# A decoder block in fp32: the raw weights of the third block get a pair of tiles of their own, in the place of a part of h2 that no product reads

## The chip, the cores and the metric

The kernel runs on one core of a Trainium2 chip. A core has a matrix engine (TensorE, PE), a vector engine (VectorE, DVE), an activation engine (ScalarE, ACT), a general engine (GpSimd, POOL) and an engine that here only issues transfers (SyncE, SP), all with their own queue of instructions, which is worked through in order. They wait for each other on semaphores. Data lies in an on-chip memory of 128 partitions (SBUF); matmuls write into banks of a second one (PSUM). The metric is the device time of one execution in microseconds (us); less is better.

## The reference

The input x has 512 tokens of width 1024. One layer:

```python
h = rmsnorm(x, norm_attn_g)
u_q, u_k, u_v, u_pool, u_gate = split(h @ w_in)
a = diff_attention(u_q, u_k, u_v, positions, lam, subln_g)
p = multiscale_pool(u_pool, w_pool, pool_scale)
gates = sigmoid(u_gate)
x = x + (gates[0] * a + gates[1] * p) @ w_out
h2 = rmsnorm(x, norm_mlp_g)
z = square(relu(h2 @ w_up))          # w_up: 1024 x 4096
x = x + z @ w_down                   # w_down: 4096 x 1024
return rmsnorm(x, final_norm_g)
```

All of it is fp32, and the result has to agree with a fp32 computation.

## The kernel before

Each fp32 operand of a large product is split into a high part, a cast to the matrix engine's float32r, and a low part, the rest of it. A product is then three matmuls: high with high, high with low, low with high. A weight tile of 128 x 1024 is loaded by SP into a raw tile, cast by ACT (`split_w`, line 112), and DVE subtracts the cast from the raw tile (line 113). High parts lie in tiles named `wh`, low parts in `wl`, four of each in rotation; every third weight of the MLP uses two others.

The first 303 us are projections, attention and pooling, and up to 353 us the product with `w_out`. The rest is the MLP, in four quarters q = 0 to 3 of the hidden width. A quarter has a product `up` (line 718), which gives z, and a product `down` (line 801), which is added to x. Both are done by Strassen's scheme in Winograd's form: the operands are cut into 2 x 2 blocks, and seven products of half the size take the place of eight. The seven forms of an operand are called A11, A12, A22 and the sums S1, S2, S3, S4. The block A21 has no product of its own: it only goes into the sums.

- For `up`, the left operand is h2. `gab[0]` holds the high and low part of A11, and in its second half those of A21; `gab[1]` holds A12 and A22; `gss` holds the sums. The loop at line 616 takes both column blocks of each of the four token tiles (t = 0 to 3), casts them (ACT, L618) and subtracts (DVE, L619). So t = 2 and 3 with b = 0 give A21. The sums are made from other tiles (`hw`, `h2f`), by `forms_h2`.
- For `down`, the left operand is z. `zsplit` casts a form of z on ACT (L705) and subtracts on DVE (L708), from tiles (`rawz`) that ACT's L757 and L758 (relu, square) and DVE's L753 have made.
- The weights come from `weights` (line 632). Of the four blocks of a quarter, three are used in raw form: r11 (b = 0), b21 (b = 2, for form A12) and b22 (b = 3, for form S4). `raw` loads each as two tiles of 128 x 1024 (512 KB each) into tiles of the tag `wr`, of which there is one pair. So the load of b21 has to wait until r11 has been cast and subtracted, and that of b22 until b21 has. The sums of blocks, `ga` and `al` (tiles `wga`, `wal`), are made by DVE (L673) and by transfers of POOL that add to the tile which they write (L643). Weights made of them are named `wh_dt` and `wh_ut`; those of raw blocks `wh_db` and `wh_ub` (d for down, u for up).
- `parts` takes a `hold`: an instruction behind which the cast is put. For b11 and b21 of `down` it is the cast of z in form S1.
- In the last quarter, b22's low part is made in another way: ACT casts (L659) and negates (L660), and POOL adds the block from memory (L661).

The order of the instructions on each engine is set by a scheduler ahead of the run, from the dependences, the tiles that come free, and a few ordering hints (`after`). SP issues all raw loads in one queue, so a load that waits for its tile stands ahead of all later ones.

`xl`, the low part of the normed x in the first projections, lies in the same memory (slot s1) that `gab[0]` takes later.

Of the kernel before, what the change touches and what calls it, by code (L numbers as in the profile page):

```python
# [18 lines left out]
P = 128  # L19
S = 512  # L20
# [31 lines left out]
def block_kernel(ctx, tc, xT, x_tok, gains, pos, consts, w_in, w_v, w_pool, w_out, w_up, w_dn, out):  # L52
# [74 lines left out]
    def mm3(acc, hi, lo, rh, rl):  # L127

        for k in range(NK):
            c = slice(k * P, (k + 1) * P)  # L130
            T.matmul(acc, lhsT=hi[:, c], rhs=rh[:, k, :], start=k == 0, stop=False)  # L131
            T.matmul(acc, lhsT=hi[:, c], rhs=rl[:, k, :], start=False, stop=False)  # L132
        for k in range(NK):
            c = slice(k * P, (k + 1) * P)
            T.matmul(acc, lhsT=lo[:, c], rhs=rh[:, k, :], start=False, stop=k == NK - 1)  # L135
# [8 lines left out]
    subc = con[:, 56:57]  # L144
    posi = cf.tile([P, NT], I32, name="posi")
    xh = B16(0, F32R, "xh")
    xl = B16(1, F32R, "xl")

    ident = cp.tile([P, P], F32, name="ident")
    make_identity(nc, ident)  # L150
# [24 lines left out]
    def xprep(k):  # L175
        xt = gt0[:, k % 4, :]
        nc.sync.dma_start(out=xt, in_=xT[k])
        A.activation(out=xh[:, k, :], in_=xt, func=AF.Copy, scale=g1c[:, k : k + 1])
        V.scalar_tensor_tensor(
            out=xl[:, k, :], in0=xt, scalar=g1c[:, k : k + 1], in1=f(xh)[:, k, :],  # L180
            op0=ALU.mult, op1=ALU.subtract,
        )

# [18 lines left out]
    for n in range(2):  # L202
        accs = [bank(4 * n + t, f"v{n}_{t}") for t in range(NT)]
        for kk in range(4):
            if n == 0:
                xprep(2 * kk)
            if n == 0 and kk == 0:
                raw, hi, lo = wv0
                nc.sync.dma_start(out=raw[:, 512:], in_=w_v[0, 0, :, 512:])
            else:  # L210
                raw, hi, lo = load_w(w_v[n, kk], f"v{n}_{kk}", 2 if n == 0 else 1)
            for k2 in range(2):
                if n == 0 and k2 == 1:
                    xprep(2 * kk + 1)
                sl = slice(k2 * 512, k2 * 512 + 512)
                split = split_w(raw, hi, lo, sl, eng=V)
                k = 2 * kk + k2
                for t in range(NT):
                    tsl = slice(t * P, t * P + P)
                    T.matmul(accs[t], lhsT=xh[:, k, tsl], rhs=hi[:, sl], start=k == 0, stop=False)  # L220
                    T.matmul(accs[t], lhsT=xh[:, k, tsl], rhs=lo[:, sl], start=False, stop=False)  # L221
                    T.matmul(accs[t], lhsT=xl[:, k, tsl], rhs=hi[:, sl], start=False, stop=k == NK - 1)  # L222
                if n == 0:
                    after(xsquare(k), split)
        if n == 0:
            pr = bank(4, "pr")
            T.matmul(pr, lhsT=ones, rhs=ssx, start=True, stop=True)
            rsqrt(rb, pr, tmp("sq", "nt1"), D)
            A.mul(out=rb, in_=rb, mul=-0.5)
            pc = bank(5, "pc")  # L230
            for t in range(NT):
                T.matmul(pc[:, 2 * t : 2 * t + 2], lhsT=ssx[:, t * P : t * P + P], rhs=ones[:, 0:2], start=True, stop=True)
            rct = cf.tile([P, NT, 2], F32, name="rct")
            rsqrt(rcol, pc[:, 0:8].rearrange("p (a b) -> p a b", a=NT), rct, D)
            A.mul(out=rcol, in_=rcol, mul=-0.5)
        for t in range(NT):
            vd = [v_[:, 4 * n : 4 * n + 4, t * P : t * P + P] for v_ in (vh, f(vh), vl)]
            av = accs[t].rearrange("p (h d) -> p h d", h=4)
            A.activation(out=vd[0], in_=av, func=AF.Copy, scale=rcol[:, t, 0:1])
            V.scalar_tensor_tensor(  # L240
                out=vd[2], in0=av, scalar=rcol[:, t, 0:1], in1=vd[1],
                op0=ALU.mult, op1=ALU.subtract,
            )
# [276 lines left out]

    h2f = zf("h2f", F32)

    gab = [big.tile([P, 2, 2, 4, HS], F32R, tag=f"s{i}", name=f"gab{i}") for i in (1, 4)]
    gss = [big.tile([P, 2, 2, 4, HS], F32R, tag=f"s{i}", name=f"gss{i}") for i in (2, 3)]
    gf = {}
    for form, g_, j in ((A11, gab[0], 0), (A12, gab[1], 0), (A22, gab[1], 1), (S1, gss[0], 0), (S2, gss[0], 1), (S3, gss[1], 0), (S4, gss[1], 1)):
# [68 lines left out]
    for t in range(NT):  # L595
        a_ = bank(4 + t, f"po1_{t}")
        for k in range(NK):
            mm_rows(a_, t, k, ws[k // 2], k == 0, k == NK - 1)
        x1_add(t, 1, a_)
        V.scalar_tensor_tensor(out=h2[:, t % 2], in0=x1[:, t, :], scalar=row_scale(t, 1), in1=g2b, op0=ALU.mult, op1=ALU.mult)  # L600
        pv = []
        for b in range(2):
            pt = bank((t % 2) * 2 + b, f"h2T{t}_{b}")
            for j in range(4):
                k = 4 * b + j
                state["h2T"] = T.transpose(out=pt[:, j * P : j * P + P], in_=h2[:, t % 2, k * P : k * P + P], identity=ident)
            pv.append(pt.rearrange("p (j q) -> p j q", q=P))
        sl = slice((t % 2) * P, (t % 2) * P + P)
        if t > 1:

            A.copy(out=hw[:, 1, :, sl], in_=pv[0])
            V.tensor_tensor(out=hw[:, 0, :, sl], in0=pv[1], in1=hw[:, 1, :, sl], op=ALU.subtract)
            forms_h2((S1, S2), sl)
        if t == 3:
            forms_h2((S3,), slice(0, HS))
        for b in range(2):
            hi, lo = (gab[b][:, t // 2, i, :, sl] for i in range(2))
            A.copy(out=hi, in_=pv[b])  # L618
            part = V.tensor_tensor(out=lo, in0=pv[b], in1=f(hi), op=ALU.subtract)  # L619
            if t == 3:  # L620
                after(part, state[S3])
            if t < 2:
                A.copy(out=h2f[:, b, :, sl], in_=pv[b])
# [8 lines left out]
    def weights(src, q, nm, order):  # L632

        def raw(b, tag="wr", pool=wp):
            tiles = [pool.tile([P, 1024], F32, tag=tag, name=f"{tag}_{nm}{b}_{q}_{c}", bufs=2) for c in range(2)]
            if b is not None:
                for c in range(2):
                    nc.sync.dma_start(out=tiles[c], in_=src[q, b, c])
            return tiles

        def plus(tiles, b):

            return [G.dma_start(out=tiles[c], in_=src[q, b, c], accum_op=ALU.add) for c in range(2)]  # L643

        def parts(rs, b, hold=None, add=None):

            third = nparts[0] % 3 == 2
            nparts[0] += 1
            out_ = []
            for c in range(2):  # L650
                hi, lo = (
                    (bk if third else wp).tile([P, 1024], F32R, tag=t_ + "b" * third, name=f"{t_}_{nm}{b}_{q}_{c}", bufs=2 if third else 4)
                    for t_ in ("wh", "wl")
                )
                if add is None:
                    cast = split_w(rs[c], hi, lo, eng=V)
                else:

                    cast = A.copy(out=hi, in_=rs[c])  # L659
                    A.mul(out=lo, in_=f(hi), mul=-1.0)  # L660
                    G.dma_start(out=lo, in_=src[q, add, c], accum_op=ALU.add)  # L661
                if hold:
                    after(cast, hold)
                out_.append((hi, lo))
            return out_

        early = nm == "u" and q == 0
        r11, al, ga = raw(0), raw(1, "wal", bk), raw(None, "wga", bk)
        for c in range(2):
            if early:  # L670
                nc.sync.dma_start(out=ga[c], in_=src[q, 0, c])
            else:
                V.tensor_tensor(out=ga[c], in0=r11[c], in1=al[c], op=ALU.add)  # L673
        if early:
            plus(ga, 1)
            plus(al, 3)
        for n, form in enumerate(order):
            if form == A11:
                yield parts(r11, "b11", zhi[q, S1] if nm == "d" and q else None)
            elif form == A12:  # L680
                yield parts(raw(2), "b21", zhi[q, S1] if nm == "d" else None)
            elif form == S4:
                yield parts(raw(3), "b22", None, 3 if nm == "d" and q == 3 else None)
            elif form == S3:
                yield parts(al, "t3", first[-1])
            else:
                w = parts(ga, f"t{form}", state["rows"] if form == S1 and early else None if form == S1 else first[-1])
                if form != A22:
                    adds = plus(ga, {S1: 3, S2: 2}[form])
                if form == S1 and not early:  # L690

                    for i in plus(al, 3):
                        after(i, adds[1])
                yield w
# [271 lines left out]
```

## Time and profile before

| what | us |
|---|---|
| runs (three) | 687.55, 687.97, 690.27 |
| median | 687.97 |
| the profiled execution's own time | 693.66 |
| its span, first to last instruction | 691.9 |

The mean clock that was granted to TensorE in the profiled execution is 0.992 of full speed. A page of the profile gives busy times and shares of the span of each engine. The weight loads of the matrix engine (PEld) run beside its matmuls. `L112` in a row is line 112 of the kernel, and the names behind it are the tiles: out, an arrow, in. Two products of `up` with different blocks have the same line; the tiles tell them apart. Rows of the timeline give the start in us from the start of the span, the duration, and in brackets the idle time of the engine ahead of the row and what ended it. What ends an idle time is inferred from semaphores; where several are waited for, the row names one of them.

### The profile page before, as it was taken

To read this page: it belongs to the slowest core of one execution; us is meant where nothing else is said; L and a number is where in the kernel's file an instruction comes from. 1 tells how busy PE (TensorE), PEld (TensorE's weight loads), DVE (VectorE), ACT (ScalarE), POOL (GpSimd) and SP (SyncE) were. 2 spreads that over 40 slices of the span, in tenths; PEclk is the share of its full clock that TensorE was granted. 3 is DMA by queue.
4 is the path that set the end of the run, shared out by engine and by line. 5 is a ranking of instruction groups with operands and counts; after the bars stand their busy time and mean duration, and the time that the engine had idled before them with its cause. 6 is when DMAs were issued, how large, how long until landed. Compare 5 with 4: busy or idle time off the path is not lost.

```text
span 691.9 us, 10006 instructions
## 1 busy us (share of the span) xinstructions
PE 670.4 (97%) x3686; PEld 581.5 (84%) x3686; DVE 516.8 (75%) x847; ACT 460.0 (66%) x741; POOL 171.1 (25%) x169
## 2 busy tenths in 40 slices
PE   8999999999999999999999999999999999989985
PEld 7788878887888888888889988999789987989764
DVE  6953977688778865965578999468894789646875
ACT  7554487877888688874578766366734776357665
POOL 6101634265346525510211020302111011202020
PEclk9999999999999999999999999999999999999998
DMA  8534473426345274564948486958669487675873
GB/s 271 180 121 114 131 152 108 112 63 153 98 124 137 77 182 90 125 209 157 288 114 172 133 195 182 204 178 178 160 195 233 133 196 213 152 176 144 213 138 121
DMA packets 32593, 109.34 MB, mean 158 GB/s; under 512 B 4001, under 2 KB 4641, under 8 KB 32545
## 3 DMA queue, kind: packets, MB, share of 16 engines
q0 software_dynamic: 10656, 38.80, 31.5%
q1 hardware_dynamic: 21744, 69.64, 29.2%
q8 instruction: 29, 0.48, 0.3%
q10 hardware_dynamic: 144, 0.26, 0.1%
q14 instruction: 20, 0.16, 0.1%
HBM read 106.59 MB, written 2.10 MB: 157 GB/s over the span
## 4 chain that ended last, share of the span: by engine, by line
PE 44%; issue 30%; DMA 16%; DVE 5%; ACT 3%; POOL 1%; SPq 0%; POOLq 0%; DVEq 0%; ACTq 0%
DMA wga_uNone<-w_up 10%; DMA wga_dNone<-w_dn 3%; PE v L220 2%; PE v L222 2%; PE gp L131 2%; PE gp L132 2%; PE gp L135 2%; PE v L221 2%; PE k L135 2%; PE o L393 2%; PE k L132 2%; PE k L131 2%; PE q L131 2%; PE q L132 2%; PE q L135 2%
## 5 line engine op out<-in xcount | busy, mean ns | idle before, releaser
L643 POOL DMA_DIRECT2D wga_dNone<-w_dn x16 | 14.2, 887 | 172.0 <-DVE wl_dt L113 172.0
L112 ACT CAST wh_ut<-wga_uNone 128x1024 fp32r<-128x1024 f32 x24 | 25.1, 1054 | 42.0 <-DMA wga_uNone<-w_up 29.7
L813 PE MATMUL dm<-wh_dt,z 128*128 128x512 f32 (+1 forms) x128 | 49.3, 386 | 0.0
L814 PE MATMUL dm<-wl_dt,z 128*128 128x512 f32 (+1 forms) x128 | 49.1, 386 | 0.0
L811 PE MATMUL dm<-wh_dt,z 128*128 128x512 f32 (+1 forms) x128 | 49.0, 387 | 0.0
L734 PE MATMUL um<-gss,wh_ut 128*128 128x256 f32 x192 | 48.2, 283 | 0.0
L732 PE MATMUL um<-gss,wh_ut 128*128 128x256 f32 x192 | 48.0, 284 | 0.2 <-ACT rawz L749 0.2
L113 DVE TENSOR_TENSOR wl_ut<-wga_uNone,wh_ut 128x1024 fp32r<-128x1024 f32 x24 | 29.2, 1226 | 20.4 <-ACT wh_ut L112 16.7
L376 ACT ACTIVATE p<-p,st 128x128 f32<-128x128 f32 (+3 forms) x64 | 35.8, 560 | 12.4 <-DVE st L372 11.8
L643 POOL DMA_DIRECT2D wga_uNone<-w_up x18 | 15.6, 867 | 113.3 <-DVE wl_ut L113 78.2
L113 DVE TENSOR_TENSOR wl_ub<-wr_u,wh_ub 128x1024 fp32r<-128x1024 f32 x24 | 29.2, 1224 | 16.3 <-ACT wh_ub L112 16.3
L829 DVE TENSOR_TENSOR x<-x,dm 128x512 f32<-128x512 f32 x48 | 32.4, 686 | 11.4 <-PE dm L814 11.2
L814 PE MATMUL dm<-wl_db,z 128*128 128x512 f32 x96 | 37.3, 399 | 2.0 <-DMA wl_db<-w_dn 2.0
L811 PE MATMUL dm<-wh_db,z 128*128 128x512 f32 x96 | 36.7, 401 | 2.3 <-ACT z L705 1.7
L112 ACT CAST wh_db<-wr_d 128x1024 fp32r<-128x1024 f32 x22 | 22.7, 1051 | 23.8 <-DMA wr_d<-w_dn 16.7
L813 PE MATMUL dm<-wh_db,z 128*128 128x512 f32 x96 | 37.1, 397 | 0.6 <-DVE z L708 0.6
L732 PEld LDWEIGHTS um<-gss,wh_ut 128*128 128x128 f32 x192 | 36.6, 192 | 0.5 <-ACT rawz L749 0.4
L734 PEld LDWEIGHTS um<-gss,wh_ut 128*128 128x128 f32 x192 | 36.8, 192 | 0.1
L732 PE MATMUL um<-gab,wh_ub 128*128 128x256 f32 x128 | 33.7, 292 | 2.1 <-ACT wh_ub L112 2.1
L112 ACT CAST wh_ub<-wr_u 128x1024 fp32r<-128x1024 f32 x24 | 25.0, 1051 | 14.7 <-DMA wr_u<-w_up 12.6
L112 ACT CAST wh_dt<-wga_dNone 128x1024 fp32r<-128x1024 f32 x24 | 24.7, 1049 | 14.9 <-DMA wga_dNone<-w_dn 5.1
L734 PE MATMUL um<-gab,wh_ub 128*128 128x256 f32 x128 | 33.6, 291 | 0.7 <-DVE gab L619 0.7
(303 smaller groups left out, 2264.9 us busy)
## 6 DMA issues: line engine op xcount, KB each, us to landing
wr_u<-w_up SPq DMA_DIRECT2D x24, 512.0 KB, 4.7
wr_d<-w_dn SPq DMA_DIRECT2D x24, 512.0 KB, 3.5
wga_uNone<-w_up POOLq DMA_DIRECT2D x18, 512.0 KB, 7.5
wga_dNone<-w_dn POOLq DMA_DIRECT2D x16, 512.0 KB, 5.7
wr_q<-w_in SPq DMA_DIRECT2D x8, 512.0 KB, 3.3
wr_k<-w_in SPq DMA_DIRECT2D x8, 512.0 KB, 3.3
wr_ga<-w_in SPq DMA_DIRECT2D x8, 512.0 KB, 3.3
wr_gp<-w_in SPq DMA_DIRECT2D x8, 512.0 KB, 3.3
```

The lines of the kernel that those rows point to most:

```text
L112: ins = A.copy(out=hi[:, sl], in_=raw[:, sl])
L113: (eng or G).tensor_tensor(out=lo[:, sl], in0=raw[:, sl], in1=f(hi)[:, sl], op=ALU.subtract)
L131: T.matmul(acc, lhsT=hi[:, c], rhs=rh[:, k, :], start=k == 0, stop=False)
L132: T.matmul(acc, lhsT=hi[:, c], rhs=rl[:, k, :], start=False, stop=False)
L135: T.matmul(acc, lhsT=lo[:, c], rhs=rh[:, k, :], start=False, stop=k == NK - 1)
L376: A.activation(out=pr[:, c, :N], in_=pr[:, c, :N], func=AF.Exp, scale=-1.0, bias=st[:, c : c + 1], accum_out=st[:, 2 + c : 3 + c])
L732: m = T.matmul(a_, lhsT=hi[:, c], rhs=rh[:, k, :], start=p + k == 0 and onto is None, stop=False, skip_group_check=True)
L734: T.matmul(a_, lhsT=hi[:, c], rhs=rl[:, k, :], start=False, stop=False, skip_group_check=True)
L811: m = T.matmul(a_, lhsT=zh, rhs=hi[:, sl], start=p == 0 and start, stop=False, skip_group_check=True)
L813: T.matmul(a_, lhsT=zl, rhs=hi[:, sl], start=False, stop=False, skip_group_check=True)
L814: end = T.matmul(a_, lhsT=zh, rhs=lo[:, sl], start=False, stop=p == 3, skip_group_check=True)
L829: V.tensor_tensor(out=xs, in0=xs, in1=pa[a], op=(ALU.add, ALU.subtract)[n])
```

## The change

The memory of slot s1 is cut into two halves, s1a and s1b. `xl` becomes two tiles, one in each. `gab[0]` shrinks to the half that A11 needs, in s1a. The casts and subtractions that gave A21 are left out. In s1b, b21's two raw tiles get a place of their own, as the two halves of one tile, `wr21`. The pair of the tag `wr` then serves r11 and b22 only. At last, the hold of b21's cast in `down` is the cast of z in form A11 in the place of form S1, and there is none in the first quarter.

```diff
-    xl = B16(1, F32R, "xl")
+    xls = [big.tile([P, 4, S], F32R, tag=f"s1{i}", name=f"xl{i}") for i in "ab"]
+    xl = [xls[k // 4][:, k % 4, :] for k in range(NK)]
...
-    gab = [big.tile([P, 2, 2, 4, HS], F32R, tag=f"s{i}", name=f"gab{i}") for i in (1, 4)]
+    gab = [big.tile([P, j, 2, 4, HS], F32R, tag=t_, name=f"gab{j}") for j, t_ in ((1, "s1a"), (2, "s4"))]
...
-        for b in range(2):
+        for b in range(t // 2, 2):
             hi, lo = (gab[b][:, t // 2, i, :, sl] for i in range(2))
             A.copy(out=hi, in_=pv[b])
             part = V.tensor_tensor(out=lo, in0=pv[b], in1=f(hi), op=ALU.subtract)
...
         def raw(b, tag="wr", pool=wp):
-            tiles = [pool.tile([P, 1024], F32, tag=tag, name=f"{tag}_{nm}{b}_{q}_{c}", bufs=2) for c in range(2)]
+            if b == 2:
+                both = big.tile([P, 2, 1024], F32, tag="s1b", name=f"wr21_{nm}{q}")
+                tiles = [both[:, c] for c in range(2)]
+            else:
+                tiles = [pool.tile([P, 1024], F32, tag=tag, name=f"{tag}_{nm}{b}_{q}_{c}", bufs=2) for c in range(2)]
...
             elif form == A12:
-                yield parts(raw(2), "b21", zhi[q, S1] if nm == "d" else None)
+                yield parts(raw(2), "b21", zhi[q, A11] if nm == "d" and q else None)
```

The rest of the diff only writes `xl[k]` for `xl[:, k]`. The lines behind these stand six further down in the changed kernel (L705 is L711 there, L757 is L763). No transfer is added or taken away.

The scheduler's order shows what moves. In the rows below, a number in a tile's name behind the quarter is the half (0 or 1), and the last one tells tiles apart that have the same name.

SP, the loads from up to down of q = 1. Before, the first `wr_u` pair is b21 of up, the second one b22; the first `wr_d` pair is r11 of down, the second b21:

```order
L638 DMA wr_u_1_0_4451<-w_up 128x1024
L638 DMA wr_u_1_1_4452<-w_up 128x1024
L638 DMA wal_d_1_0_4610<-w_dn 128x1024
L638 DMA wal_d_1_1_4611<-w_dn 128x1024
L638 DMA wr_u_1_0_4522<-w_up 128x1024
L638 DMA wr_u_1_1_4523<-w_up 128x1024
L638 DMA wr_d_1_0_4606<-w_dn 128x1024
L638 DMA wr_d_1_1_4607<-w_dn 128x1024
L638 DMA wr_d_1_0_4694<-w_dn 128x1024
L638 DMA wr_d_1_1_4695<-w_dn 128x1024
```

After, where `wr_u_1_0_4516` and its twin are b22 of up, `wr_d_4688` is b21 of down, `wr_d_1_0_4600` r11 and `wr_d_1_0_4759` b22 of down:

```order
L644 DMA wr_u_1_0_4516<-w_up 128x1024
L644 DMA wr_u_1_1_4517<-w_up 128x1024
L644 DMA wal_d_1_0_4604<-w_dn 128x1024
L644 DMA wal_d_1_1_4605<-w_dn 128x1024
L644 DMA wr_d_4688<-w_dn 128x1024 x2
L644 DMA wr_d_1_0_4600<-w_dn 128x1024
L644 DMA wr_d_1_1_4601<-w_dn 128x1024
L644 DMA wr_d_1_0_4759<-w_dn 128x1024
L644 DMA wr_d_1_1_4760<-w_dn 128x1024
```

b22 of up now has the place of b21 of up, b21 of down that of b22 of up, and b22 of down that of b21 of down. b21 of the next quarter's up stands behind these rows.

ACT in down of q = 1, before, from the cast of z in form A11 (the first L705) to the casts of the first accumulated weight (`wh_dt`). `wh_db_1_0_4698` and `wh_db_1_1_4702` are the casts of b21; the second L705 is z in form A12:

```order
L705 CAST z_1_4519<-rawz 128x1024
L758 ACTIVATE rawz<-rawz 128x512
L757 ACTIVATE rawz<-rawz 128x512
L758 ACTIVATE rawz<-rawz 128x512
L112 CAST wh_db_1_0_4698<-wr_d_1_0_4694 128x1024
L705 CAST z_1_4588<-rawz 128x1024
L705 CAST z_1_4592<-rawz 128x1024
L112 CAST wh_db_1_1_4702<-wr_d_1_1_4695 128x1024
L112 CAST wh_dt_1_0_4730<-wga_dNone_0_4614 128x1024
L112 CAST wh_dt_1_1_4734<-wga_dNone_1_4615 128x1024
```

After:

```order
L711 CAST z_1_4513<-rawz 128x1024
L112 CAST wh_db_1_0_4691<-wr_d_4688 128x1024
L112 CAST wh_db_1_1_4695<-wr_d_4688 128x1024
L764 ACTIVATE rawz<-rawz 128x512
L763 ACTIVATE rawz<-rawz 128x512
L764 ACTIVATE rawz<-rawz 128x512
L711 CAST z_1_4582<-rawz 128x1024
L711 CAST z_1_4586<-rawz 128x1024
L112 CAST wh_dt_1_0_4723<-wga_dNone_0_4608 128x1024
L112 CAST wh_dt_1_1_4727<-wga_dNone_1_4609 128x1024
```

Both casts of b21 have moved ahead of the relu and square that z in form A12 is made by. In q = 2 it is the same. In q = 0 they also move ahead of casts of z.

ACT at the end of q = 3, before, from the loading of the final gain to the second L660. `wh_db_3_0_6269` and `wh_db_3_1_6274` are the two halves of b22:

```order
L534 ACTIVATE gfb<-gfb 128x1024
L112 CAST wh_dt_3_0_6229<-wga_dNone_0_6103 128x1024
L112 CAST wh_dt_3_1_6233<-wga_dNone_1_6104 128x1024
L705 CAST z_3_6082<-rawz 128x1024
L705 CAST z_3_6086<-rawz 128x1024
L659 CAST wh_db_3_0_6269<-wr_d_3_0_6265 128x1024
L660 ACTIVATE wl_db_3_0_6270<-wh_db_3_0_6269 128x1024
L112 CAST wh_dt_3_0_6325<-wal_d_3_0_6099 128x1024
L659 CAST wh_db_3_1_6274<-wr_d_3_1_6266 128x1024
L112 CAST wh_dt_3_1_6329<-wal_d_3_1_6100 128x1024
L705 CAST z_3_6089<-rawz 128x1024
L660 ACTIVATE wl_db_3_1_6275<-wh_db_3_1_6274 128x1024
```

After:

```order
L536 ACTIVATE gfb<-gfb 128x1024
L112 CAST wh_dt_3_0_6218<-wga_dNone_0_6093 128x1024
L112 CAST wh_dt_3_1_6222<-wga_dNone_1_6094 128x1024
L665 CAST wh_db_3_0_6258<-wr_d_3_0_6254 128x1024
L665 CAST wh_db_3_1_6263<-wr_d_3_1_6255 128x1024
L666 ACTIVATE wl_db_3_0_6259<-wh_db_3_0_6258 128x1024
L666 ACTIVATE wl_db_3_1_6264<-wh_db_3_1_6263 128x1024
L711 CAST z_3_6072<-rawz 128x1024
L711 CAST z_3_6076<-rawz 128x1024
L112 CAST wh_dt_3_0_6314<-wal_d_3_0_6089 128x1024
L112 CAST wh_dt_3_1_6318<-wal_d_3_1_6090 128x1024
L711 CAST z_3_6079<-rawz 128x1024
```

Both halves of b22 are cast and negated right behind the `wh_dt` casts. On POOL the last four transfers were `wga` half 0, `wl_db` half 0, `wga` half 1, `wl_db` half 1; now both of `wl_db` stand ahead of the second `wga`.

More of the change, by code (lines that the diff above doesn't have):

```diff
@@ L131, in mm3 @@
             T.matmul(acc, lhsT=hi[:, c], rhs=rh[:, k, :], start=k == 0, stop=False)
-            T.matmul(acc, lhsT=hi[:, c], rhs=rl[:, k, :], start=False, stop=False)
+            T.matmul(acc, lhsT=hi[:, c], rhs=rl[k], start=False, stop=False)
         for k in range(NK):
@@ L179, in xprep @@
         V.scalar_tensor_tensor(
-            out=xl[:, k, :], in0=xt, scalar=g1c[:, k : k + 1], in1=f(xh)[:, k, :],
+            out=xl[k], in0=xt, scalar=g1c[:, k : k + 1], in1=f(xh)[:, k, :],
             op0=ALU.mult, op1=ALU.subtract,
@@ L221, in block_kernel @@
                     T.matmul(accs[t], lhsT=xh[:, k, tsl], rhs=lo[:, sl], start=False, stop=False)
-                    T.matmul(accs[t], lhsT=xl[:, k, tsl], rhs=hi[:, sl], start=False, stop=k == NK - 1)
+                    T.matmul(accs[t], lhsT=xl[k][:, tsl], rhs=hi[:, sl], start=False, stop=k == NK - 1)
                 if n == 0:
```

## The prediction, made before the changed kernel was run

> **What bounds the kernel now.** I read the page first, then the waits of TensorE (PE) from 303 us on, then the timeline of each engine that is named there.
>
> ```profile
> PE 670.4 (97%) x3686; PEld 581.5 (84%) x3686; DVE 516.8 (75%) x847; ACT 460.0 (66%) x741; POOL 171.1 (25%) x169
> ```
>
> PE is busy for 670.4 us of a span of 691.9 us, and the change takes no matmul away. So all that it can win is time in which PE waits or runs slowly. Where PE waits in the out-projection and the MLP, the waits view (engine, line, what was waited for: total, times, longest, in us) says in full:
>
> ```profile
> PE um L732 <- ACT wh_ub L112: 2.1, 1, 2.1
> PE dm L814 <- DMA wl_db<-w_dn: 2.0, 1, 2.0
> PE dm L811 <- ACT z L705: 1.7, 2, 0.9
> PE um L732 <- DVE rawz L753: 0.7, 1, 0.7
> PE um L734 <- DVE gab L619: 0.7, 1, 0.7
> PE dm L813 <- DVE z L708: 0.6, 1, 0.6
> PE dm L811 <- ACT wh_db L112: 0.6, 1, 0.6
> PE um L732 <- ACT rawz L749: 0.2, 1, 0.2
> ```
>
> Nine waits, 8.6 us together. The timeline of PE places them (start, duration, then in brackets the idle time ahead and its releaser):
>
> ```profile
> 354.58 0.38 PE L734 MATMUL um<-gab,wh_ub 128*128 128x256 f32 x1 [0.67 <-DVE gab L619]
> ...
> 386.43 0.38 PE L732 MATMUL um<-gab,wh_ut 128*128 128x256 f32 x1 [0.72 <-DVE rawz L753]
> ...
> 488.62 0.50 PE L813 MATMUL dm<-wh_db,z 128*128 128x512 f32 x1 [0.61 <-DVE z L708]
> 492.90 0.73 PE L811 MATMUL dm<-wh_db,z 128*128 128x512 f32 x2 [0.82 <-ACT z L705]
> ...
> 572.80 0.74 PE L811 MATMUL dm<-wh_db,z 128*128 128x512 f32 x2 [0.88 <-ACT z L705]
> ...
> 619.00 0.58 PE L732 MATMUL um<-gab,wh_ub 128*128 128x256 f32 x1 [2.15 <-ACT wh_ub L112]
> ...
> 654.14 0.50 PE L811 MATMUL dm<-wh_db,z 128*128 128x512 f32 x1 [0.57 <-ACT wh_db L112]
> ...
> 666.70 0.79 PE L814 MATMUL dm<-wl_db,z 128*128 128x512 f32 x1 [2.00 <-DMA wl_db<-w_dn]
> ```
>
> Those of 488 to 493, 572 and 654 lie in the down products of q = 1, 2 and 3 and name ACT or DVE. ACT's own timeline says why it was late. In q = 1:
>
> ```profile
> 479.54 0.63 ACT L757 ACTIVATE rawz<-rawz 128x512 f32<-128x512 f32 x1 [0.76 <-DVE rawz L753]
> 480.21 0.63 ACT L758 ACTIVATE rawz<-rawz 128x512 f32<-128x512 f32 x1
> 485.11 1.05 ACT L112 CAST wh_db<-wr_d 128x1024 fp32r<-128x1024 f32 x1 [4.27 <-PE dm L814]
> 486.07 1.99 ACT L705 CAST z<-rawz 128x1024 fp32r<-128x1024 f32 x2
> ```
>
> ACT stands still for 4.27 us ahead of the first cast of b21, and the two casts of z that PE asks for are behind it. The row names PE, but the tile's view shows a load that was just then landing:
>
> ```profile
> L638 SPq DMA_DIRECT2D wr_d<-w_dn x4: 327/328/328, 476.1 to 492.6; - x4
> DMA to landing us min/median/max: 3.3/6.1/9.4
> ```
>
> The first of these four is b21's, issued at 476.1 us; some 9 us (the longest landing is 9.4) end at 485. It could not be issued sooner, since r11 held the one pair of raw tiles. Likewise in q = 2 and q = 3:
>
> ```profile
> 564.95 1.06 ACT L112 CAST wh_db<-wr_d 128x1024 fp32r<-128x1024 f32 x1 [3.68 <-DMA wr_d<-w_dn]
> ```
>
> ```profile
> 649.27 1.05 ACT L112 CAST wh_db<-wr_d 128x1024 fp32r<-128x1024 f32 x1 [2.73 <-PE dm L814]
> 653.04 1.05 ACT L112 CAST wh_db<-wr_d 128x1024 fp32r<-128x1024 f32 x1 [2.72 <-DMA wr_d<-w_dn]
> ...
> 658.74 1.07 ACT L659 CAST wh_db<-wr_d 128x1024 fp32r<-128x1024 f32 x1
> 659.84 1.06 ACT L660 ACTIVATE wl_db<-wh_db 128x1024 fp32r<-128x1024 f32 x1
> ```
>
> **The change, part by part.** *The loads.* With a pair of its own, b21 no longer waits for r11, and b22 takes the place behind r11 that b21 had. In SP's order the loads of one quarter were r11, b21, b22 of up, then r11, b21, b22 of down, each behind the subtraction of the one before it. Now b22 goes where b21 went, and b21 of down goes where b22 of up went, behind the subtraction of b21 of up. So the moments at which SP moves 1 MB stay nearly the same; only what is moved changes. That is why I put no new contention of DMAs into the sum. In q = 1 the moments for the two halves of b21 of down are those of the first two rows, which were b22 of up (SP's timeline):
>
> ```profile
> 452.86 0.33 SPq L638 DMA_DIRECT2D wr_u<-w_up x1
> ...
> 458.95 0.33 SPq L638 DMA_DIRECT2D wr_u<-w_up x1
> 460.68 0.33 SPq L638 DMA_DIRECT2D wr_d<-w_dn x1
> ```
>
> Adding the longest landing, 9.4 us, both halves are there by 468.4 us, 10 us ahead of ACT's L757 at 479.54. SP's queue is strictly in order, so the waiting load of b21 stands ahead of r11 of down; r11 went out at 460.68 us before (the third row), after both of these moments, so nothing is held up. The queue of POOL keeps its order but for q = 3.
>
> *Down of q = 1, 2, 3.* ACT casts b21 right behind z of A11, ahead of L757 and L758 of z's A12. Both casts add 2 us ahead of that z, but the wait of 4.27 us goes: z of A12, which was cast at 486.07, comes after L758's old end at 480.84 plus 2.0 us, at about 483. The wait at 488.62 and that at 492.90 hang on this chain, so 0.61 + 0.82 = 1.43 us go. What is late next is DVE's subtraction for the same z; following DVE's queue I place its end at 486.5 us, 1.5 us ahead of the 488.0 at which PE was free. In q = 2 the same gives 0.88 us and in q = 3 0.57 us. Bounds for the three: nothing (the casts still late) to 2.88 us; I take the upper end, because ACT's waits that go, 4.27, 3.68 and 5.45 us, are several times as long as PE's.
>
> *End of q = 3.* b22's low half is made by ACT (L659, L660) and an accumulating DMA of POOL (L661):
>
> ```profile
> 661.19 5.46 DMA wl_db<-w_dn
> ```
>
> The row is from the chain of waits: 5.46 us from this DMA's issue at 661.19 to 666.65 us, which is where PE's 2.00 us end. Now b22's raw is loaded where b21's was, so it is there at about 649 and 653 us, ACT has lost its two waits of 2.73 and 2.72 us, and both casts and both L660 stand ahead of z's S3 and S4 casts. Four operations of about 1 us behind the wh_dt casts put the first DMA at about 656 us and its landing, 5.5 us on, at 661.5; the two halves now run beside each other, so I allow 2.5 us more for the second. PE's need moves forward too, by the waits that vanish ahead of it, to about 663. So I take the 2.00 us as gone, with a margin of 1 to 2 us. With it goes a slow stretch behind the wait:
>
> ```profile
> 667.29 0.63 PE L811 MATMUL dm<-wh_db,z 128*128 128x512 f32 x1
> ...
> 670.41 0.39 PE L814 MATMUL dm<-wl_db,z 128*128 128x512 f32 x1
> ...
> 671.34 0.39 PE L813 MATMUL dm<-wh_dt,z 128*128 128x512 f32 x1
> ```
>
> ```profile
> 667.00:670.10 3.10, 3.10 (x8) 2.42 (x8) 2.92 (x6) 1.79 (x3) 0.00 (x0) 0.51 1.05 200
> 670.10:676.00 5.90, 5.90 (x27) 4.86 (x27) 2.52 (x3) 0.94 (x3) 0.00 (x0) 1.00 0.19 38
> ```
>
> In the windows view (time, PE, weight loads, DVE, ACT, POOL, granted clock, DMA share, GB/s) the clock is 0.51 in the first stretch and 1.00 in the next. Nine matmuls start from 666.70 to 670.41, 3.71 us; at the pitch behind it, (671.34 - 670.41)/4 = 0.23 us, they take 2.09. So the half clock costs 1.62 us, and this place is worth 3.62 us, nothing if the landing stays late. The six shorter waits, up to 0.88 us, show no such stretch. [...]
>
> *Up of q = 0.* b21's load goes out ahead of x_tok's, and no longer behind r11, wal and wga of up. Here ACT waited for it:
>
> ```profile
> 350.29 1.05 ACT L112 CAST wh_ub<-wr_u 128x1024 fp32r<-128x1024 f32 x1 [0.99 <-DMA wr_u<-w_up]
> ```
>
> The casts of gab and, through them, DVE's L619 stand behind, so they come up to 0.99 us sooner, and the 0.67 us at 354.58 go (bounds nothing to 0.67).
>
> *The part of h2 left out.* Two casts on ACT (L618) and two subtractions on DVE (L619) are gone. Only one lies where an engine is waited for:
>
> ```profile
> 378.81 1.28 DVE L619 TENSOR_TENSOR gab<-h2T,gab 128x512 fp32r<-128x512 f32 x2
> ...
> 385.68 0.69 DVE L753 TENSOR_TENSOR rawz<-um,rawz 128x512 f32<-128x512 f32 x1
> ```
>
> DVE works without a pause from the first row to the second, which is what PE waits for at 386.43. One of the two L619 goes, 0.6 us; of PE's 0.72 us I take 0.6 (bounds nothing to 0.72).
>
> *What costs nothing.* xl in two tiles holds the same data, and the matmuls read it the same way. The wait of 2.15 us at 619.00 stays: ACT's b21 cast is there behind casts that wait for an accumulating DMA, and neither that order nor that DMA changes.
>
> *Sum.* 0.67 + 0.6 + 1.43 + 0.88 + 0.57 + 3.62 = 7.8 us. Against it stands the risk of new waits. The thinnest place is down of q = 0, where both b21 casts move ahead of casts of z with about half a microsecond to spare, by my count. I allow one wait of the size of the short ones here (0.57 to 0.88), 0.8 us. Left: 7.0 us of the profiled execution's 693.66 us (the span of 691.9 us and 1.8 us around it), or 1.0%. The median of the runs is 687.97 us, 5.7 us below that execution; 1.0% off it is **681 us**.
>
> **The rivals.** *The casts come no sooner than before.* Each also needs the tile that it writes, which PE frees with the last product of up. Then only 0.67 + 0.6 us go, 1.3: 686.7 us. Against it: L757 at 479.54 already had that product's sum, 5.6 us ahead of the cast at 485.11. Chance 0.1, no change.
>
> *The waits belong half to the profiled execution.* It is 5.7 us slower than the runs, and waits on loads may be shorter there, or other short waits take their place one for one. With half of 7.0 us, 684.5 us; this is the edge of 0.5%, which is 3.4 us and about what a measurement of this kernel can tell from no change. Chance 0.2.
>
> *Slower: the b21 cast blocks ACT earlier.* It now stands ahead of L757 and L758, which were done by 480.84. If b21's load landed at 485 as before, both casts (2.0 us) and then L758, L757, L758 (1.9 us) would come ahead of z: its cast would start at about 489 and not at 486.07, 3 us later. Each of three quarters would lose 3 us and, from 2 us of wait on, 1.6 us of half clock: 14 us less the 1.3 won elsewhere, 700 us. It decides at a landing after 479.54, so an issue after 470.1 us; the subtraction that it waits for came 11 us before that. Chance 0.06.
>
> **How the numbers follow.** The forecast, all or nearly all of the 7.0 us, has 0.64. The case of half the gain counts one half as faster and one half as no change: faster 0.64 + 0.1 = 0.74, same 0.1 + 0.1 = 0.2, slower 0.06. The range's low end has no new wait and also the wait at 619.00 shortened by 2 us, 677.5 us; its high end takes in the case of half the gain and the first rival, 687 us.
>
> **What would show it.** In the changed kernel's trace: no idle time of ACT ahead of wh_db casts near 480, 560 and 645 us; no wait for wl_db and a granted clock of 1.00 near 662 us; L619 x6; DVE's run ahead of 386 shorter by 0.6 us; the wait of some 2 us near 615 still there. The forecast is wrong if PE waits for z in down of q = 0, if ACT waits for b21's load, or if PE idles behind the wh_dt casts of the accumulated weights.

## The result, and the profile after

The changed kernel takes 678.79 us (median of four runs, 677.76 to 679.05) against 688.89 us for the kernel before in the same comparison. The ratio is 0.985 with a 95% interval of 0.9825 to 0.9876, so it saves 10.1 us (8.5 to 12.1). A second comparison gave 0.9847 (0.9827 to 0.9867). The forecast was 681 us and 7.0 us saved: the sign is right and the size is 3 us short.

The page of the changed kernel, and its waits of PE from 303 us on, which are an empty list (the two lines are the view's heading):

```profile
PE 665.5 (98%) x3686; PEld 579.0 (86%) x3686; DVE 514.8 (76%) x845; ACT 460.8 (68%) x739; POOL 170.8 (25%) x169
```

```profile
core 0 of [0], span 677.1 us
engine line waited for: us in total, times, longest us
```

All nine waits of before are gone, the one that the forecast had left standing among them. ACT's timeline of the changed kernel in down of q = 1, and at the end of q = 3:

```profile
474.13 1.04 ACT L711 CAST z<-rawz 128x1024 fp32r<-128x1024 f32 x1
475.07 2.00 ACT L112 CAST wh_db<-wr_d 128x1024 fp32r<-128x1024 f32 x2
476.97 0.63 ACT L764 ACTIVATE rawz<-rawz 128x512 f32<-128x512 f32 x1
...
478.82 2.00 ACT L711 CAST z<-rawz 128x1024 fp32r<-128x1024 f32 x2
...
643.54 1.05 ACT L665 CAST wh_db<-wr_d 128x1024 fp32r<-128x1024 f32 x1 [1.11 <-DMA wr_d<-w_dn]
644.50 2.00 ACT L666 ACTIVATE wl_db<-wh_db 128x1024 fp32r<-128x1024 f32 x2
```

Both casts of b21 stand right behind z's form A11, with no idle time in brackets. z's form A12 starts at 478.82 us, directly behind its square. The prediction expected no idle time of ACT ahead of the casts near 480, 560 and 645 us. That holds for b21, not for b22: at the end of q = 3 ACT waits 1.11 us for its second half, and it idles ahead of b22's first cast in q = 1 (1.73 us at 484.45) and q = 2 (2.18 us at 562.91). PE waits for none of them. POOL's transfers for b22 then go out far earlier than at 661.19:

```profile
645.84 1.81 POOL L667 DMA_DIRECT2D wl_db<-w_dn  x2 [0.67 <-ACT wl_db L666]
```

The two profiled executions differ by 14.6 us (693.66 and 679.05 us), more than the medians. The first experiment says why.

### The profile page after: what moved, and what is told of

Its sections match the earlier page's. It is cut to its first block, busy times and chain, and to the rows that moved or that the text cites. A ratio compares the mean times of both kernels' runs of the same rounds, so it can differ in the third digit from the quotient of the medians.

```text
span 677.1 us, 10004 instructions
## 1 busy us (share of the span) xinstructions
PE 665.5 (98%) x3686; PEld 579.0 (86%) x3686; DVE 514.8 (76%) x845; ACT 460.8 (68%) x739; POOL 170.8 (25%) x169
## 4 chain that ended last, share of the span: by engine, by line
PE 77%; DVE 8%; DMA 5%; ACT 5%; issue 4%; SPq 0%; POOL 0%; DVEq 0%; ACTq 0%; POOLq 0%
PE dm L817 7%; PE dm L819 7%; PE dm L820 7%; PE um L738 7%; PE um L743 7%; PE um L740 7%; DMA wga_uNone<-w_up 4%; PE gp L131 2%; PE gp L132 2%; PE gp L135 2%; PE k L135 2%; PE k L132 2%; PE k L131 2%; PE q L131 2%; PE q L132 2%
## 5 line engine op out<-in xcount | busy, mean ns | idle before, releaser
L714 DVE TENSOR_TENSOR z<-rawz,z 128x1024 fp32r<-128x1024 f32 x28 | 33.6, 1215 | 0.5 <-ACT z L711 0.5
L740 PE MATMUL um<-gab,wh_ub 128*128 128x256 f32 x128 | 32.4, 284 | 0.0
L738 PE MATMUL um<-gab,wh_ub 128*128 128x256 f32 x128 | 32.1, 283 | 0.0
```

Of the source, the lines that this page charges most:

```text
L714: V.tensor_tensor(out=z[:, 1], in0=r, in1=f(z[:, 0]), op=ALU.subtract)
L738: m = T.matmul(a_, lhsT=hi[:, c], rhs=rh[:, k, :], start=p + k == 0 and onto is None, stop=False, skip_group_check=True)
L740: T.matmul(a_, lhsT=hi[:, c], rhs=rl[:, k, :], start=False, stop=False, skip_group_check=True)
```

## The experiments

Theory A says that ACT's wait for b21 in `down` is the root of nearly all that vanished, also of the wait at 619 us in the next quarter's `up`, to which it is carried on. The rival, B, says that the wait at 619 went because b21 of `up` is loaded earlier and out of the way of POOL's accumulating transfers. Each ratio is against runs of the kernel before in the same comparison. Line numbers are those of the changed kernel, except in runs of before.

### The kernel before, once more

No edit.

> The kernel before once more, as it is, to see which of PE's waits belong to the kernel and which to one execution. If the nine waits of the first profile are the kernel's own, they come back within 0.3 us each, 8.6 us together, with a half clock behind the two of 2 us, and the span is about 690 us. The other view: the four runs without a profile (687.55 to 690.27) are 3.4 to 6.1 us below the profiled one (693.66) because one or both of the waits of 2 us, each worth some 3.7 us with its half clock, come in only some executions. Then one or both of 619.00 and 666.70 are gone or much shorter here, and the seven short waits are back.

Ratio 1.0006 (0.9977 to 1.0035). The profiled execution took 688.86 us. PE's waits from 303 us on, and the windows view of the 3.1 us behind the wait for `wl_db` (the granted clock is the third number from the end):

```profile
core 0 of [0], span 687.1 us
...
PE dm L814 <- DMA wl_db<-w_dn: 2.0, 1, 2.0
PE um L732 <- ACT wh_ub L112: 1.6, 1, 1.6
PE dm L811 <- ACT z L705: 1.3, 2, 0.9
PE um L732 <- DVE rawz L753: 0.7, 1, 0.7
PE dm L811 <- ACT wh_db L112: 0.5, 1, 0.5
PE um L734 <- DVE gab L619: 0.3, 1, 0.3
```

```profile
663.40:666.50 3.10, 3.10 (x14) 2.57 (x15) 3.10 (x9) 1.88 (x4) 0.07 (x1) 1.00 1.03 194
```

Seven of the nine waits are back, 6.4 us in the place of 8.6. The same wait of 2.0 us has no half clock behind it this time, and 14 matmuls in 3.1 us where the first profile had 8. Behind the 1.6 us the clock is 1.00 as well (616.70 to 620.00). So neither reading was wholly right: the long waits belong to the kernel, and their half clocks to single executions. The 25 runs of before in this comparison go from 686.89 to 694.02 us. The first profile, at 693.66, lies near the upper end of that spread; its distance to the median is not the price of profiling, as the forecast's second rival supposed.

### Only the unread part of h2 left out

```diff
-            if b == 2:
+            if False:
...
-                yield parts(raw(2), "b21", zhi[q, A11] if nm == "d" and q else None)
+                yield parts(raw(2), "b21", zhi[q, S1] if nm == "d" else None)
```

> Only the casts and subtractions of the part of h2 that no product reads are left out; b21 shares the pair of raw tiles with r11 and b22 as before, and its hold is the old one. By the prediction's sum this is worth 0.6 us: the wait near 386 goes from 0.72 to about 0.1, and all of the others stay (354.58 by 0.67, those of the down products, 619 and 667). If instead ACT's and DVE's two instructions less help elsewhere, 1 us or more.

Ratio 0.9988 (0.9962 to 1.0014), so 0.8 us less, between 2.6 less and 1.0 more. The trace has no wait near 386 us any more. The waits for `wh_ub` (1.5 us at 616.6) and for `wl_db` (1.7 us at 662.5) are still there, and so are those of 354 (0.6 us), 492 (1.1) and 571 (0.35). Not all stayed, as was expected: that of 654 is missing, and a second one for `wl_db` has come (1.1 us at 669.0). The term of 0.6 us fits; time alone can't confirm one so small.

### Tiles of its own in `down` only, in `up` only

```diff
-            if b == 2:
+            if b == 2 and nm == "d":
```

> b21 has its own tiles in the down products only; in up it shares the pair with r11 and b22. Theory A (one late wait is carried on): the wait of 2.15 us at 619 came from ACT's wait for b21 in down of q = 2, through ACT's casts of wh_dt, POOL's accumulating DMAs and DVE's backlog; so here it is gone, as are those of 488 to 493, 572, 654 and 667, and the 0.67 us at 354 stay. Time within 1.5 us of the changed kernel. Rival B (traffic): the wait at 619 went because b21 of up is loaded earlier, away from the accumulating DMAs of up; then 2 us with a half clock, 3.7 us, are back near 610 here.

> b21's own tiles in the down products only, again, beside the changed kernel on the same chip: what is the tile in up worth? By the prediction the 0.67 us at 354.58 (0.1%); by the first run of this kernel, where PE waited 0.49 us there and nowhere else, 0.5 us. If up's earlier loads also ease the traffic of the accumulating DMAs, more than 1.5 us.

Ratios 0.9857 (0.9809 to 0.9905) and 0.9856 (0.9834 to 0.9879), beside 0.9847 of the changed kernel in the second comparison. The whole list of PE's waits in the first profile:

```profile
PE um L740 <- DVE gab L621: 0.5, 1, 0.5
```

The mirror image, with the old hold:

```diff
-            if b == 2:
+            if b == 2 and nm == "u":
...
-                yield parts(raw(2), "b21", zhi[q, A11] if nm == "d" and q else None)
+                yield parts(raw(2), "b21", zhi[q, S1] if nm == "d" else None)
```

> The mirror: b21 has its own tiles in the up products only, and the old hold. Theory A: the waits of the down products and those of 619 and 667 all stay, and only those of 354 (0.67) and 386 go, so it is 1 to 2 us faster than before. Rival B: the wait at 619 goes too, 4 to 6 us faster than before.

Ratio 1.0023 (0.9995 to 1.0052). Its waits, and the clock behind the third:

```profile
PE dm L820 <- DMA wl_db<-w_dn: 4.4, 1, 4.4
PE dm L819 <- DVE z L714: 2.7, 3, 1.1
PE um L738 <- ACT wh_ub L112: 1.8, 1, 1.8
```

```profile
617.00:620.00 3.00, 3.00 (x15) 3.00 (x16) 3.00 (x5) 2.25 (x3) 0.00 (x0) 0.51 0.00 0
```

With the tile in `down` only, the wait at 619 is gone; with the tile in `up` only, it is there (1.8 us). That is what A says, and B falls. Tiles in `up` only were expected to save 1 to 2 us and save nothing: the waits at 354 and 386 did go, but the one for `wl_db` grew to 4.4 us in the profiled execution. It is for POOL's second transfer, which was issued at 660.55 us and took 8.91 us, against 5.46 for the first one in the kernel before. Why it took so long was not followed up. What the tile in `up` adds to that in `down` is, in the two profiles, the wait at 354 (0.5 and 0.7 us); the ratios, 0.0009 apart, don't resolve it.

### One quarter alone: shared in q = 2, and own in q = 2

The changed kernel, with b21 of `down` back in the shared pair in q = 2 alone:

```diff
-            if b == 2:
+            if b == 2 and (nm, q) != ("d", 2):
...
-                yield parts(raw(2), "b21", zhi[q, A11] if nm == "d" and q else None)
+                yield parts(raw(2), "b21", zhi[q, S1 if q == 2 else A11] if nm == "d" and q else None)
```

> The changed kernel, but in down of q = 2 alone b21 shares the pair as before, with its old hold; up of q = 3 is the changed kernel's. Theory A: ACT waits some 3.7 us for b21 in down of q = 2, the 0.9 us of PE near 565 come back, and 18 to 25 us after down's start of the next quarter's up, near 612, a wait of 1 to 2.5 us ahead of the first product with wh_ub comes back too, although nothing was changed there: 2 to 4.5 us slower than the changed kernel. Rival B: only the 0.9 us come back.

And the converse, in which only q = 2 of `down` has the tiles and the new hold:

```diff
-            if b == 2:
+            if b == 2 and (nm, q) == ("d", 2):
...
-                yield parts(raw(2), "b21", zhi[q, A11] if nm == "d" and q else None)
+                yield parts(raw(2), "b21", zhi[q, A11 if q == 2 else S1] if nm == "d" else None)
```

> The converse: as before (b21 shares the pair, old hold, the unread part of h2 left out), but in down of q = 2 alone b21 has its own tiles and the new hold. Theory A: the 0.88 us near 572 go and the 2.15 us near 619 go with them, with their half clock; the waits of q = 1 (488 to 493) and those of q = 3 (654, 667) stay: 4 to 6 us faster than before, counting 0.6 for the part of h2. Rival B: 619 stays, 1 to 2 us faster than before.

Ratios 0.9867 (0.9846 to 0.9888) and 0.9946 (0.9924 to 0.9968). PE's waits, first of the one that shares in q = 2, then of the one that has its own there:

```profile
PE um L738 <- ACT wh_ub L112: 1.9, 1, 1.9
```

```profile
PE dm L820 <- DMA wl_db<-w_dn: 2.0, 1, 2.0
PE dm L817 <- ACT z L711: 0.8, 1, 0.8
PE um L740 <- DVE gab L621: 0.7, 1, 0.7
```

This settles where the wait begins. Sharing in `down` of q = 2 alone brings back the wait ahead of `wh_ub` in `up` of q = 3, whose code is untouched, and no other. Owning in `down` of q = 2 alone removes that wait and the one near 572, and leaves one of q = 1 and the 2.0 us at the end. (The wait at 654 is not in this list, though b21 shares the pair in q = 3 here.) The steps between are read from the rows. How a late cast gets there is seen on POOL: the last accumulating transfer of the first pair (`wga_d`), the first of the second pair, and the last of the next `up` (`wga_u`). Shared, with two rows of ACT behind it:

```profile
547.57 0.87 POOL L649 DMA_DIRECT2D wga_dNone<-w_dn  x1 [3.14 <-DVE wl_dt L113]
...
568.56 0.86 POOL L649 DMA_DIRECT2D wga_dNone<-w_dn  x1 [18.34 <-DVE wl_dt L113]
...
600.54 0.86 POOL L649 DMA_DIRECT2D wga_uNone<-w_up  x1 [1.60 <-DVE wl_ut L113]
```

```profile
559.09 1.05 ACT L112 CAST wh_db<-wr_d 128x1024 fp32r<-128x1024 f32 x1 [4.12 <-DMA wr_d<-w_dn]
...
610.92 1.04 ACT L112 CAST wh_ut<-wga_uNone 128x1024 fp32r<-128x1024 f32 x1 [2.80 <-DMA wga_uNone<-w_up]
```

Own:

```profile
550.44 0.86 POOL L649 DMA_DIRECT2D wga_dNone<-w_dn  x1 [3.14 <-DVE wl_dt L113]
...
565.92 0.86 POOL L649 DMA_DIRECT2D wga_dNone<-w_dn  x1 [12.83 <-DVE wl_dt L113]
...
600.52 0.86 POOL L649 DMA_DIRECT2D wga_uNone<-w_up  x1 [0.27 <-DVE wl_ut L113]
```

ACT's wait of 4.12 us delays its casts of `wh_dt` behind it, and so the next transfer into `wga_d`: 20.99 us after the first row when shared, 15.48 when owned. Half of that is still there a quarter later: the last transfer into `wga_u` goes out after 52.97 us against 50.08. It lands for the cast at 610.92, 10.4 us on, and the cast of b21 that PE needs is queued behind it on ACT. The kernel before shows the same pattern: 553.88, 573.83 and 606.44 us in its POOL rows, 19.95 and 52.56 us apart from the first. All thirteen traces of this case fall in line with it: the two distances are 19.8 to 22.7 and 52.3 to 54.7 us in the six in which b21 shares the pair in `down` of q = 2, 15.5 to 16.3 and 50.1 to 50.9 us in the six in which it has its own tiles there, and 17.3 and 52.0 us in the one in which r11 has them (below).

```profile
553.88 0.86 POOL L643 DMA_DIRECT2D wga_dNone<-w_dn  x1 [3.14 <-DVE wl_dt L113]
...
573.83 0.86 POOL L643 DMA_DIRECT2D wga_dNone<-w_dn  x1 [17.30 <-DVE wl_dt L113]
...
606.44 0.86 POOL L643 DMA_DIRECT2D wga_uNone<-w_up  x1 [1.56 <-DVE wl_ut L113]
```

Two expectations of A were too large. Sharing in q = 2 cost about 1 us over the changed kernel's ratio, with intervals that overlap, and not 2 to 4.5: the wait had no half clock in the profiled execution (granted clock 1.00 from 613.00 to 616.40 us), and PE's 0.9 us in `down` did not return, though ACT was late by 4.12 us. Owning there saved 3.7 us (2.2 to 5.2), just below the 4 to 6 expected; the interval holds a part of both.

### The old hold; r11 in the place of b21

```diff
-                yield parts(raw(2), "b21", zhi[q, A11] if nm == "d" and q else None)
+                yield parts(raw(2), "b21", zhi[q, S1] if nm == "d" else None)
```

> All of the change but the hold: b21's cast in down stays held behind the cast of z in form S1 (as before), which lets the scheduler put it ahead of z in form A11. If the tiles alone do the work, within 1 us of the changed kernel, no wait above 0.5 us in the down products. If the hold matters, z in form A11 comes up to 2 us late (two casts of 1 us ahead of it), and PE waits for it in each down product: 1 to 3 us slower than the changed kernel.

Ratio 0.9906 (0.9871 to 0.994). PE's waits:

```profile
PE dm L820 <- DMA wl_db<-w_dn: 0.7, 1, 0.7
PE dm L819 <- DVE z L714: 0.2, 1, 0.2
```

With the tiles alone, the waits of q = 1 and q = 2 go as well. The first expectation holds for the trace but for 0.7 us at the end of q = 3. The ratio is higher by 0.0056 than the changed kernel's, some 4 us. The intervals just meet in the changed kernel's first comparison and just miss in its second, and one of the four runs here, 685.3 us against 680.67 to 681.87, carries part of the difference. By the spans of the profiled executions, 678.9 against 677.1 us, it is 1.8 us. How much the hold is worth stays open; these two numbers give some 4 and some 2 us.

```diff
-            if b == 2:
+            if b == 0:
```

> The same memory given to r11 in the place of b21, in up and down; b21 and b22 share the pair. b21 of down can then load as soon as b22 of up has been subtracted, near 460 us in q = 1 and some 15 us before its cast. Theory A: any tile that brings b21 of down in time removes the late waits and what they carry on, so this is within 2 us of the changed kernel, and 619 and 667 are gone. If it matters that b21 and not r11 has the tile, b22 in turn is late (it waits for b21 to be subtracted) and PE waits for it in the down products, 0.5 to 1 us each.

Ratio 0.9872 (0.9849 to 0.9894). Its waits:

```profile
PE um L740 <- DVE gss L582: 0.9, 1, 0.9
PE um L738 <- ACT gss L581: 0.3, 1, 0.3
```

The same memory spent on r11 does nearly as well: no wait in any `down`, none at 619 or at the end, and two in `up` of q = 0, 1.2 us together. So it is a second buffer for one of the two early loads that counts, not which of them has it; PE does not wait for b22.

### The slower rival: b21's casts ahead of z, with the shared pair

```diff
-            if b == 2:
+            if False:
...
+                state.setdefault("relu", []).append(ins)
...
                 if hold:
                     after(cast, hold)
+                if nm == "d" and b == "b21" and q:
+                    after(state["relu"][-1], cast)
```

> The prediction's slower rival, made on purpose: b21 shares the pair as before (the unread part of h2 left out), but in q = 1 to 3 both of its casts in down are put ahead of the last square for z in form A12. The rival says that ACT then waits for the load (until about 485 to 488 us in q = 1), z in form A12 starts some 3 us later than before, and PE waits 3 us longer in each of the three quarters, at times with a half clock: 6 to 14 us slower than before. If PE has more slack there than I counted, less than 4 us slower.

Only the last square is put behind the casts here, where the rival counted three operations (1.9 us), so this is a milder form of it. Ratio 1.0071 (1.0043 to 1.01): 4.9 us slower than before. PE's waits, and ACT in q = 3:

```profile
PE dm L820 <- ACT z L713: 6.3, 3, 3.8
PE dm L822 <- DVE z L716: 1.7, 3, 0.7
PE dm L823 <- DMA wl_db<-w_dn: 1.0, 1, 1.0
PE um L742 <- DVE gab L621: 0.5, 1, 0.5
```

```profile
647.18 1.05 ACT L112 CAST wh_db<-wr_d 128x1024 fp32r<-128x1024 f32 x1 [5.98 <-DMA wr_d<-w_dn]
...
650.67 2.00 ACT L713 CAST z<-rawz 128x1024 fp32r<-128x1024 f32 x2
```

The mechanism is real: without the load in time, casts that stand ahead of z make PE wait for z. But a price of 3 us or more comes in q = 3 alone (3.8 us); q = 1 has 0.9 and then 0.5 us, together as much as before, and q = 2 has 1.6 and 0.5. The prediction's 12.7 us (14 less 1.3) were 4.9 (3.0 to 6.9). The wait for `wh_ub` in `up` is not in this list although b21 is late. The lateness was carried on all the same: the two distances on POOL are 22.74 and 54.73 us, the largest of all traces. But PE had itself lost 2.1 us in `down` of q = 2. It ended the product ahead of `wh_ub` at 616.62 us, when the first of the two casts, begun at 615.59, was just done.

### The changed kernel again

> The changed kernel, on the chip of the next two runs and against the same runs of before, for a narrower ratio. If the waits of PE that vanished are the whole of it, their sum without half clocks (6.4 us of idle time in the second profile of before, 0.1 here) and the end behind the last matmul (about 1 us) give a ratio near 0.988; with half clocks in many executions of before, 0.983 to 0.986.

Ratio 0.9847 (0.9827 to 0.9867), and again an empty list of waits. It lies where the second branch put it, in which a part of the executions of before has half clocks; how many have them was not counted.

```profile
core 0: 677.6 us, clock 0.948
```

The clock of this execution reads 0.948 in the view of the cores, where the other three runs have 0.997 to 0.999, and the time is the same (679.54 us beside 678.54 to 679.38). What the record means here is open.

## Why the prediction was right, and where it was short

*The bound* was read rightly: the change takes no matmul away, and what it gained is PE's idle and slow time.

*Down of q = 1 to 3* (2.88 us): right. The cause was the load behind ACT's wait, not PE or the z casts that the rows name, and all of these waits went. The size varies; the second profile of before has 1.8 us of them. ACT's wait alone doesn't set it: with b21 late in q = 2, PE lost 0.88 us in both profiles of before and 0.35 without the unread part of h2, and nothing with q = 2 alone shared. For the 0.57 us of q = 3 it stays open, since that wait is missing in two runs that share the pair there.

*The end of q = 3* (3.62 us): the 2.00 us went as worked out. The 1.62 us of half clock were mis-sized as a term of the kernel: the second profile has the same wait at full clock (granted clock 1.00, where the first has 0.51). For a median such a term counts with the share of executions that have it.

*The wait at 354* (0.67 us) and *that at 386* (0.6): right; the latter went wholly with the left-out part of h2 alone, and the former stays, at 0.3 to 0.7 us, in the traces in which `up` has the shared pair alone.

*"The wait of 2.15 us at 619.00 stays"*: this step failed. It looked at the order of that place and at the transfer next to it, both unchanged, but not at when the chain that ends there begins. It begins in `down` of the quarter before, at ACT's wait for b21. The two runs with q = 2 alone show it from both sides.

*New waits*, 0.8 us: none came. The thin margin in `down` of q = 0 held.

Adding the two last, 7.0 + 2.15 + 0.8 = 9.95 us, beside 10.1 measured. That is closer than the parts deserve, since half clocks come and go. From the second profile of before it reads: 10.0 us between the spans, of which 6.4 are waits of PE, 0.9 lie behind the last matmul (its start is 8.0 us ahead of the span's end before, 7.1 after), 0.5 lie ahead of 303 us, and the other 2.2 or so are lost at the waits beyond their idle time (the starts of the same matmuls compared). The 0.9 us were not followed up.

```profile
679.07 0.28 PE L814 MATMUL dm4b<-wl_dt,z 128*128 128x256 f32 x1
```

```profile
669.99 0.28 PE L820 MATMUL dm4b<-wl_dt,z 128*128 128x256 f32 x1
```

*The rivals.* The casts did come sooner. The waits were not an effect of profiling: seven of the nine came back in a profiled execution of 688.86 us, below the median of its kernel's runs. The slower rival's place was right. Its price was more than twice what its milder form cost: q = 1 lost no more than before and q = 2 1.2 us more, so PE had more slack there than was counted.

## What to carry to other kernels

An engine that works its queue in order and waits for one late load delays more than the next product: follow what it does afterwards (casts, transfers, the other engines' backlog) for as long as it takes, with q = 2 alone shared for 54 us and into the next quarter (from ACT's cast at 559 us to the end of PE's wait of 1.9 us at 613), before a wait elsewhere is called independent. A second profile of the kernel before tells which waits belong to the kernel and which, with their slow clock, to one execution. When three loads take turns in one buffer pair, a second buffer for one of them can be enough; here it was so for b21 and for r11, and b22 was not tried.

## What the runs showed of the hardware

A wait of PE of about 2 us was followed by a stretch at half clock in one execution and not in the next. In the first profile of before, the granted clock was 0.50 for 3.3 us behind the wait of 2.15 us (618.95 to 622.25) and for 3.4 us behind that of 2.00 us (666.65 to 670.05); from 622.30 and from 670.10 us on it was 1.00 again. Behind the wait of 2.0 us in the second profile it was 1.00 (663.40 to 666.50), and behind the 1.8 us with b21's tiles in `up` only it was 0.51 (617.00 to 620.00). Behind the 1.9 us with q = 2 alone shared it was 1.00 (613.00 to 616.40), and behind the 2.0 us with q = 2 alone owned as well (658.70 to 662.00). So in these six the length of the wait alone doesn't decide: 1.8 us had a half clock behind it, and 1.9 and 2.0 us had none. What decides was not shown; no run varied one property of such a wait alone.
